# Five first pairs instead of six in a two-layer GELU block: the second and third range of the first weight prepared sooner, its factors on GpSimd

## The chip, the cores and the metric

The kernel runs on one core of one Trainium2 chip. The metric is device time in microseconds (us): the median over runs of the same kernel. Engines are named as in the profile: PE is TensorE's matmul, PEld its weight load, DVE is VectorE, ACT is ScalarE, POOL is GpSimd, SP is SyncE, which here only issues DMAs.

## The reference

`x` has 8 x 1024 rows of 1024, `w1` is 1024 x 4096, `w2` is 4096 x 1024, all float32.

```python
h = x @ w1
h = 0.5 * h * (1 + np.tanh(np.sqrt(2 / np.pi) * (h + 0.044715 * h ** 3)))
return (h @ w2).astype(np.float32)
```

## The kernel before

**Tiling.** The 8192 rows are 32 pairs of two blocks of 128 rows (`NP`). The 4096 columns of `w1` are two halves, and each half is cut into four ranges of 512 columns (`NR`). The unit of the first product is one pair and one range: two row blocks by two column halves, over two halves of the 1024 inner rows. That is a 2 x 2 by 2 x 2 block product. Done plainly (class `Plain`, L511) it takes 32 matmuls of 512 columns, in four quarters of eight. Done as `Quad1` (L540) it takes seven block products, m1 to m7, of four matmuls each, and needs sums of blocks on both sides: `sum_x` (L222) for x, and T1, T2, T3, T4 of the weight, made by `sum_w1` (L362).

**A range of w1** goes through these steps before it can be used: eight tiles of 512 KB are loaded by `load_w1` (L277; ranges 1 to 3 are issued by POOL, range 0 by SP), each tile is looked at for its largest value by `look_w1` (L291, on DVE or ACT), `widest_w1` (L306, DVE) takes the maximum per partition, `scale_w1` (L314) takes it over all partitions with one PE transposition into the tile `rows` (L158) followed by a DVE reduction, `factors` (L244) makes the scales for the GELU input and output, `cast_w1` (L348) makes float16 tiles, two tiles to each of the blocks B11, B21, B12 and B22, and `sum_w1` makes the T's. T4 takes the place of B12.

**A row block of x** is loaded (`load_x`, L181, SP), looked at (`look_x`, L185, ACT), scaled and cast (`cast_x`, L196), and turned, for the first pairs by eight PE transpositions and a copy out of PSUM (`turn_x_pe`, L206), later by a DMA.

**The order.** The first `FIRST` = 6 pairs are taken range by range: units 0 to 5 are range 0 done plainly, 6 to 11 are range 1, 12 to 17 range 2, 18 to 23 range 3, all as `Quad1`. Then come 22 middle pairs with all four ranges each, then the last four pairs range by range. Range 0 is cast with scales of its own halves for the plain units, and evened out in place (`even_w1`, L340, POOL) before the middle pairs use it. After 128 units the second product, with `w2`, follows.

**What sets the order on each engine.** Everything stands in the order in which it is written, and each engine runs its own queue strictly in that order. A plain quarter p is followed by GELUs of finished quarters and then by what was put at place p with `early`. In `unit` (L796) the steps of unit u stand between background slots 0 to 6; work is put there with `plan(u, slot, ...)`. The order inside one unit, which the prediction's steps use, is: m1 and its copy (ACT); slot 0; m7 of the unit before, its copy (ACT) and its addition (DVE); GELUs; slot 1; m3 of the unit two before and an addition (DVE); slot 2; m2 and an addition (DVE); slot 3; m6 (needs T2) and its copy (ACT); GELUs; slot 4; m5 (needs T1); slot 5; m4 of the unit before (needs T4); slot 6. The function `between(p)` (L915) puts the last x blocks and the second half of range 0 into the middle of the quarters 2 to 6. At p = 2 and p = 4, x blocks 5 and 7 are cast on POOL.

In the texts below T8, T9, T10 and T11 (with "x block") are the PE transpositions of x blocks 8 to 11, and q16 is the plain quarter 16; u7 is unit 7.

Of the kernel before, what the change touches and what calls it, by code (L numbers as in the profile page):

```python
# [31 lines left out]
B11, T4, B21, B22, T1, T2, T3 = range(7)  # L32
# [48 lines left out]
def kernel(  # L81
# [19 lines left out]
    NP = T // (2 * P)  # L101
    NR = I // 2 // N
    JR = N // P
    FIRST = 6
    LAST = 4
    OPEN = 4
    WARM = 52
# [3 lines left out]
    wpool = ctx.enter_context(tc.tile_pool(name="wpool", bufs=NR * 7))  # L111
    k4 = ctx.enter_context(tc.tile_pool(name="k4", bufs=15))
    k2 = ctx.enter_context(tc.tile_pool(name="k2", bufs=11))
    k1 = ctx.enter_context(tc.tile_pool(name="k1", bufs=8))
# [9 lines left out]
    xm = small.tile([P, T // P], F32, name="xm")  # L124
    xi = small.tile([P, T // P], F32, name="xi")
# [4 lines left out]
    w1m = small.tile([P, NR + 4], F32, name="w1m")  # L130
    w1i = small.tile([P, NR + 4], F32, name="w1i")
    w1j = small.tile([P, NR + 2], F32, name="w1j")
# [6 lines left out]
    us = small.tile([P, NP, 2, NR], F32, name="us")  # L139
    rs = small.tile([P, NP, 2, NR], F32, name="rs")  # L140
    rt = small.tile([P, T // P], F32, name="rt")
    up = small.tile([P, 3, 2 * FIRST], F32, name="up")
    ratio = small.tile([P, 4], F32, name="ratio")
# [4 lines left out]
    V, S, G = nc.vector, nc.scalar, nc.gpsimd  # L148
# [89 lines left out]
    def times(o, a, s, eng=V):  # L238
        if eng is G:
            G.tensor_scalar(out=o, in0=a, scalar1=s, scalar2=1.0, op0=ALU.mult, op1=ALU.mult)  # L240
        else:
            V.tensor_scalar(out=o, in0=a, scalar1=s, scalar2=None, op0=ALU.mult)

    def factors(k0, k1, r):  # L244

        c = slice(2 * k0, 2 * k1)
        view = lambda t: t[:, k0:k1].rearrange("p k h r -> p (k h) r")[:, :, r]
        times(view(us), xm[:, c], w1m[:, r:r + 1])
        times(view(rs), xi[:, c], w1j[:, r:r + 1])

    def ups_of_block(k, eng):
        c = slice(2 * k, 2 * k + 2)
# [206 lines left out]
    class Out1:  # L459


        def begin(self, k, r):
# [4 lines left out]
            if not r:  # L467
                self.v = [[self.v[h][0], rt[:, c(h)]] for h in range(2)]
            if not r and k < FIRST:
                self.u = [[(up[:, 0, c(h)], up[:, 1, c(h)]), up[:, 2, c(h)]] for h in range(2)]  # L470
# [206 lines left out]
    NQ = len(order)  # L677
    todo = {}

    def plan(u, slot, f, *args):  # L680
        assert 0 <= u, (f, args)
        todo.setdefault((u, slot), []).append((f, args))
# [6 lines left out]
    def early(p, f, *args):  # L689
        plan(p // 4, p % 4, f, *args)  # L690

    for k in range(OPEN, FIRST):
        for h in range(2):
            c = 2 * k + h
            p = (9, 12)[k - OPEN] + h
            early(p - 1, look_x, c)
            early(p, scale_x, c)
            early(p, cast_x, c, V)
            if h:
                early(p, factors_of_block, k, 0, G)  # L700
                early(p, factors_of_block, k, 1, G)
            early((2, 5)[k - OPEN], load_x, c, wpool, "w")
            early(4 * k - 2 + 2 * h - (k > 2), turn_x_pe, c, V if h else S)
    for k in first:
        for i in range(4):
            if k < 2:
                early((18, 21)[k] + i // 2, sum_x, k, (i,))
            else:
                plan(FIRST + k - 1, 2 + i, sum_x, k, (i,))

    for n in range(8):
        early((3, 4, 5, 6, 7, 8, 9, 10)[n], load_w1, 1, n)
        early((7, 8, 10, 12, 12, 13, 14, 15)[n], look_w1, 1, n, S if n in (3, 5, 7) else V)
    early(15, widest_w1, 1)
    early(17, scale_w1, 1)
    early(17, factors, 0, FIRST, 1)
    for i, n in enumerate((4, 5, 0, 1, 6, 7, 2, 3)):
        early((17, 17, 18, 18, 19, 19, 20, 21)[i], cast_w1, 1, n, S if i % 2 and n != 3 or n == 2 else V)
    early(20, sum_w1, 1, T1)
    early(22, sum_w1, 1, T2)  # L720
    plan(FIRST, 1, sum_w1, 1, T3)
    plan(FIRST, 5, sum_w1, 1, T4)
    for r in range(2, NR):
        u = (r - 1) * FIRST - 1
        for n in range(8):
            v = u - 1 + n // 2
            if r == 2:
                plan(*((4, 1), (4, 3), (5, 0), (5, 2))[n // 2], load_w1, r, n)
                look = ((5, 3), (6, 1), (6, 1), (6, 4), (6, 3), (7, 1), (7, 1), (7, 4))[n]
                plan(*look, look_w1, r, n, S if n % 2 else V)  # L730
            else:
                plan(v, 1, load_w1, r, n)
                look = (v + 2, 1) if n == 1 else (v + 1, 3 + n % 2)
                plan(*look, look_w1, r, n, S if n == 1 else V)
        plan(u + 3, 1 if r == 2 else 5, widest_w1, r)
        plan(*((u + 3, 6) if r == 2 else (u + 4, 2)), scale_w1, r)
        plan(u + 4, 2, factors, 0, FIRST, r)
        for n in range(8):
            v, slot = ((4, 3), (4, 4), (4, 5), (5, 1), (4, 3), (4, 5), (5, 3), (4, 6))[n]
            plan(u + v, slot, cast_w1, r, n, (G, S, G, S, G, V, S, V)[n])  # L740
        for i, t in enumerate((T1, T3, T2, T4)):
            plan(u + 5 + i // 2, (4, 6, 1, 3)[i], sum_w1, r, t)
    early(10, join_w1)
    for i, b in enumerate((B12, B11, B22, B21)):
        for half in range(2):
            plan(3 * FIRST - 1 + i, (2, 5)[half], even_w1, b, half)
    for i, t in enumerate((T1, T3, T2, T4)):
        plan(3 * FIRST + 1 + i, 5, sum_w1, 0, t)

    for k in list(middle) + list(last):  # L750
        a = at[k] if k in middle else at[last[0]]
        for h in range(2):
            c = 2 * k + h
# [10 lines left out]
    u = at[middle[0]] - 1  # L764
    for ic in range(2 * IK):
        t = 7 * u + ic * 35 // 8
# [6 lines left out]
    for c in range(8):  # L773
        v = u + 2 + c * 7
# [12 lines left out]
    for i, node in enumerate(FORMS):  # L787
        r, n = divmod(i, 7)
# [52 lines left out]
    with tc.manual_schedule(  # L841
# [18 lines left out]
        for n in range(4, 8):  # L860
# [5 lines left out]
        t = x16[0]  # L866
# [8 lines left out]
        warm_up(t, 8)  # L875
        cast_w1(0, 0, V)
        cast_w1(0, 1, V)
        plain = {k: Plain(k, 0) for k in range(FIRST)}
        pa, pc = bank("pa"), bank("pc")
        plain[0].eighth(0, 0, pa)  # L880
        look_w1(0, 2, S)
        scale_x(1)
        cast_x(1, V)
# [4 lines left out]
        warm_up(t, 3)  # L888
        turn_x_pe(1, V)
        scale_w1(NR + 3)  # L890
        plain[0].eighth(1, 0, pc)
        cast_w1(0, 2, V)
        cast_w1(0, 3, S)
        ups_of_block(0, G)
# [2 lines left out]
        look_x(3)  # L897
        join_halves()
        inverse_w1(slice(NR, NR + 1), G)
        plain[0].eighth(0, 1, pa)  # L900
        turn_x_pe(2, S)
        times(rs[:, 0, :, 0], xi[:, 0:2], w1j[:, NR:NR + 1], G)
        plain[0].eighth(1, 1, pc)
        scale_x(3)
        cast_x(3, V)
        look_x(4)
        look_x(5)
        quarters = [(k, 0, half, s) for s in range(2) for k in range(OPEN) for half in range(2)]
        quarters += [(k, 0, half, s) for k in range(OPEN, FIRST) for half in range(2) for s in range(2)]
        gelus = {  # L910
            0: lambda: plain[0].gelu(0, 0, plain[0].e(), pa),
            1: lambda: plain[0].gelu(1, 0, plain[0].e(), pc),
        }

        def between(p):  # L915
            if p == 2:
                scale_x(4)
                turn_x_pe(3, V)
                cast_x(4, V)
                scale_x(5)  # L920
                cast_x(5, G)
                gelus.pop(0)()
                factors_of_block(1, 0, G)
                look_x(6)
            elif p == 3:
                turn_x_pe(4, V)
                scale_x(6)
                look_w1(0, 4)
                gelus.pop(1)()
                factors_of_block(2, 0, G)  # L930
                look_x(7)
            elif p == 4:
                turn_x_pe(5, V)
                cast_x(6, V)
                scale_x(7)
                cast_x(7, G)
                look_w1(0, 5, S)
                gelus.pop(2)()
            elif p == 5:
                turn_x_pe(6, V)  # L940
                factors_of_block(3, 0, G)
                look_w1(0, 6)
                look_w1(0, 7, S)
                widest_w1(0, 1)
                gelus.pop(3)()
            elif p == 6:
                turn_x_pe(7, V)
                scale_w1(NR + 1)
                for n in range(4, 8):
                    cast_w1(0, n, S if n % 2 else V)  # L950
                inverse_w1(slice(NR + 1, NR + 2), G)
                for k in range(OPEN):
                    factors_of_block(k, 1, G)
                gelus.pop(4)()

        for p, (k, r, half, s) in enumerate(quarters):
            if p > 1:
                gelus[p] = plain[k].quarter(half, s, ("pa", "pc")[p % 2], lambda: between(p))
            if p > 6:
                for i in list(gelus)[:2]:  # L960
                    gelus.pop(i)()
            for j in (p % 4,) if p % 4 < 3 else (3, 4, 5, 6):
                background(p // 4, j)
            let_go(len(held) - 1 if len(held) > 1 and p % 2 else 0)
        now = {}
        for u in range(FIRST, NQ):
            unit(u, None)
        V.tensor_scalar(
            out=vo, in0=xm, scalar1=w2n, scalar2=SPAN, op0=ALU.mult, op1=ALU.mult
# [38 lines left out]
```

## Time and profile before

| what | number |
|---|---|
| median of 3 runs | 1530.53 us (1530.23 to 1531.13) |
| the profiled execution's own time | 1530.9 us |
| its span, first to last instruction | 1529.1 us |
| PE busy | 1521.4 us, 99% |
| DVE busy | 1176.3 us, 77% |
| ACT busy | 738.7 us, 48% |
| POOL busy | 478.1 us, 31% |
| granted TensorE clock | 1.00 |
| chain that ended last | PE 99%, DMA 1% |
| DMA, mean | 192 GB/s over the span, 330 GB/s from 20 to 50 us |

The span is the time between the first and the last instruction; the run's own time is 1.8 us longer, and the median of the runs lies 0.4 us under that run's time. A line of a timeline has the start in us, the time from start to end, the engine, the line of the kernel, the operation, what it writes and reads, and how many instructions were merged; a bracket at its end tells how long the engine was idle before and what ended that. "SPq" is the queue of SyncE. Two neighbouring instructions of one engine can overlap by some tens of ns, so in a full queue the distance from start to start is a little less than the duration.

### The profile page before, as it was taken

Reading aid. Unit: us, or ns where it says so; the run is one execution under the profiler, and the core shown is the slowest. Engines: PE = TensorE matmul, PEld = TensorE weight load, DVE = VectorE, ACT = ScalarE, POOL = GpSimd, SP = SyncE. Lnnn points to the kernel's source line nnn. Section 1 sums busy time; section 2 is a strip of 40 time slices with the busy share of each in tenths; the row PEclk is TensorE's granted clock in tenths of the full one; section 3 lists DMA queues with packets and bytes.
Section 4 is the critical chain, followed back from the end, with each engine's and each line's share of the span. In section 5 each row is a group of like instructions: output and inputs, shape, how many; then the busy total and the mean of one; then the engine's idle time right before and its main releaser. Section 6 shows DMA issues by size and latency. Waiting matters only on the chain.

```text
span 1529.1 us, 28771 instructions
## 1 busy us (share of the span) xinstructions
PE 1521.4 (99%) x10449; PEld 1018.4 (67%) x10449; DVE 1176.3 (77%) x2404; ACT 738.7 (48%) x1322; POOL 478.1 (31%) x604
## 2 busy tenths in 40 slices
PE   8999999999999999999999999999999999999999
PEld 5444444444444444444458888888888888888888
DVE  6886788777777777574348888888888888888886
ACT  7878778777777777787662111111111111111111
POOL 4789554555666666554440000000000000000000
PEclk9999999999999999999999999999999999999999
DMA  9764989888789788875995767767766866866873
GB/s 351 237 201 141 294 259 300 251 238 249 203 238 270 225 258 232 246 201 131 287 280 128 145 135 135 152 131 132 155 138 123 162 131 125 163 134 131 151 141 81
DMA packets 460991, 293.94 MB, mean 192 GB/s; under 512 B 334000, under 2 KB 429232, under 8 KB 460848
## 3 DMA queue, kind: packets, MB, share of 16 engines
q1 hardware_dynamic: 457392, 279.52, 72.5%
q0 software_dynamic: 3456, 12.58, 2.5%
q8 instruction: 81, 1.33, 0.4%
q14 instruction: 62, 0.51, 0.1%
HBM read 96.99 MB, written 114.29 MB: 138 GB/s over the span
## 4 chain that ended last, share of the span: by engine, by line
PE 99%; DMA 1%; ACT 0%; SPq 0%; issue 0%; DVE 0%; ACTq 0%
PE pa L438 53%; PE pc L438 31%; PE pb L438 14%; DMA xn<-in_x_dram 1%; PE turned L213 0%; SPq L286 0%; ACT junk L187 0%; ACT w L172 0%; ACT xT L218 0%; PE rows L158 0%; SPq L183 0%; DVE o L626 0%; ACT junk L302 0%; DVE w1a L312 0%; ACTq L483 0%
## 5 line engine op out<-in xcount | busy, mean ns | idle before, releaser
L438 PEld LDWEIGHTS <-gs 128*128 128x128 f16 x4608 | 450.8, 98 | 53.0 <-DVE gs L168 0.2
L174 POOL TENSOR_SCALAR g<-e,rs 128x512 f16<-128x512 f32 x446 | 364.2, 826 | 280.9 <-ACT e L483 247.7
L438 PEld LDWEIGHTS <-xs 128*128 128x128 f16 x1952 | 191.0, 98 | 229.7
L165 DVE TENSOR_TENSOR e<-pc,e 128x512 f32<-128x512 f32 x244 | 162.8, 686 | 204.0 <-ACT e L577 202.9
L438 PEld LDWEIGHTS <-xT 128*128 128x128 f16 x1672 | 162.8, 98 | 193.8 <-DVE xT L220 1.7
L438 PE MATMUL pa<-w,gs 128*128 128x256 f16 x2304 | 288.3, 273 | 0.0
L438 PE MATMUL pa<-w,xT 128*128 128x512 f16 (+1 forms) x1080 | 254.7, 377 | 0.5 <-ACT xT L218 0.2
L483 ACT ACTIVATE e<-e,us 128x512 f32<-128x512 f32 x366 | 251.2, 719 | 2.1 <-DVE e L165 2.0
L438 PE MATMUL pa<-w,xs 128*128 128x512 f16 x976 | 250.5, 379 | 0.0
L438 PE MATMUL pc<-w,xs 128*128 128x512 f16 x976 | 250.5, 379 | 0.0
L438 PEld LDWEIGHTS <-gT 128*128 128x128 f16 x2048 | 200.4, 98 | 23.2
L630 ACT ACTIVATE o<-pa,vo 128x256 f32<-128x256 f32 x96 | 45.2, 471 | 332.4 <-PE pa L438 332.4
L438 PE MATMUL pc<-w,gs 128*128 128x256 f16 x1536 | 193.8, 273 | 0.0
L438 PE MATMUL pa<-w,gT 128*128 128x256 f16 x1024 | 132.7, 273 | 0.0
L438 PE MATMUL pb<-w,xT 128*128 128x512 f16 x488 | 125.2, 379 | 0.0
L626 DVE SCALAR_TENSOR_TENSOR o<-pc,vo,o 128x256 f32<-128x256 f32 x160 | 77.1, 482 | 58.0 <-PE pc L438 58.0
L568 ACT COPY e<-pa 128x512 f32<-128x512 f32 x122 | 71.4, 585 | 91.1 <-PE pa L438 86.8
L168 DVE TENSOR_TENSOR gs<-gT,gs 128x1024 f16<-128x1024 f16 x160 | 109.8, 686 | 0.9 <-DMA gT<-gd 0.9
L626 DVE SCALAR_TENSOR_TENSOR o<-pa,vo,o 128x256 f32<-128x256 f32 x192 | 92.0, 480 | 19.3 <-PE pa L438 19.0
L438 PE MATMUL pc<-w,gT 128*128 128x256 f16 x768 | 99.5, 273 | 0.0
L438 PE MATMUL pb<-w,gs 128*128 128x256 f16 x768 | 99.5, 273 | 0.0
L558 ACT COPY e<-pa 128x512 f32<-128x512 f32 x122 | 70.5, 578 | 50.0 <-PE pa L438 49.0
(105 smaller groups left out, 1443.4 us busy)
## 6 DMA issues: line engine op xcount, KB each, us to landing
gd<-g SPq DMA_DIRECT2D x504, 128.0 KB, 3.3
wn<-in_w_dram SPq DMA_DIRECT2D x72, 512.0 KB, 5.1
xn<-in_x_dram SPq DMA_DIRECT2D x64, 512.0 KB, 5.8
out_dram<-o SPq DMA_DIRECT2D x62, 512.0 KB, 3.8
w<-wd SPq DMA_DIRECT2D x25, 512.0 KB, 5.9
wn<-in_w_dram POOLq DMA_DIRECT2D x24, 512.0 KB, 6.1
wd<-wt SPq DMA_DIRECT2D x24, 512.0 KB, 4.7
gT<-gd SPq DMA_TRANSPOSE x128, 6.3
```

Of the source, the lines that this page charges most:

```text
L165: V.tensor_tensor(out=o, in0=a, in1=b, op=ALU.add)
L168: V.tensor_tensor(out=o, in0=a, in1=b, op=ALU.subtract)
L174: G.tensor_scalar(out=o, in0=i, scalar1=s, scalar2=1.0, op0=ALU.mult, op1=ALU.mult)
L438: nc.tensor.matmul(bank, lhsT=left(i), rhs=right[i], start=start and i == 0, stop=i == n - 1, skip_group_check=True,)
L483: S.activation(out=e[:, c], in_=src[:, c], func=ACT.Gelu_apprx_tanh, scale=scale)
L558: S.copy(self.e11, self.pa)
L568: S.copy(self.e12, self.pa)
L626: V.scalar_tensor_tensor(out=o, in0=ps, scalar=v, in1=o, op0=ALU.mult, op1=ALU.add)
L630: S.activation(out=o, in_=ps, func=ACT.Copy, scale=v)
```

## The change

`FIRST` becomes 5. Only ten x blocks are then turned on PE. The quarters 0 to 19 are the five pairs on range 0; the quarters 20 to 23 are new and do pair 0 on range 1 plainly, so there are still six plain units. Unit 6 is now pair 1 on range 1, and there are 23 middle pairs. Range 1 is therefore needed from quarter 20, range 2 from unit 10 (before: 12), range 3 from unit 15 (before: 18), range 0 again from unit 20 (before: 24). The steps that prepare them are put sooner, and `factors` goes from DVE to POOL for ranges 1 to 3. One cast of range 3 stays on POOL where there were three.

```diff
-    FIRST = 6
+    FIRST = 5
...
-    def factors(k0, k1, r):
+    def factors(k0, k1, r, eng=V):
...
+        times(view(us), xm[:, c], w1m[:, r:r + 1], eng)
+        times(view(rs), xi[:, c], w1j[:, r:r + 1], eng)
...
-            if k < 2:
-                early((18, 21)[k] + i // 2, sum_x, k, (i,))
+            if k == 1:
+                early(22 + i // 2, sum_x, k, (i,))
             else:
-                plan(FIRST + k - 1, 2 + i, sum_x, k, (i,))
+                plan(FIRST - 1 + (k or FIRST), 2 + i, sum_x, k, (i,))
     for n in range(8):
-        early((3, 4, 5, 6, 7, 8, 9, 10)[n], load_w1, 1, n)
-        early((7, 8, 10, 12, 12, 13, 14, 15)[n], look_w1, 1, n, S if n in (3, 5, 7) else V)
+        early((3, 3, 3, 4, 4, 5, 5, 6)[n], load_w1, 1, n)
+        early((8, 9, 10, 11, 12, 13, 14, 14)[n], look_w1, 1, n, S if n % 2 else V)
     early(15, widest_w1, 1)
-    early(17, scale_w1, 1)
-    early(17, factors, 0, FIRST, 1)
-    for i, n in enumerate((4, 5, 0, 1, 6, 7, 2, 3)):
-        early((17, 17, 18, 18, 19, 19, 20, 21)[i], cast_w1, 1, n, S if i % 2 and n != 3 or n == 2 else V)
-    early(20, sum_w1, 1, T1)
-    early(22, sum_w1, 1, T2)
-    plan(FIRST, 1, sum_w1, 1, T3)
-    plan(FIRST, 5, sum_w1, 1, T4)
+    early(15, scale_w1, 1)
+    early(15, factors, 0, FIRST, 1, G)
+    for n in range(8):
+        early(16 + n // 2, cast_w1, 1, n, S if n % 2 else V)
+    for i, t in enumerate((T1, T2, T3, T4)):
+        plan(*((4, 3), (5, 0), (5, 1), (6, 1))[i], sum_w1, 1, t)
     for r in range(2, NR):
         u = (r - 1) * FIRST - 1
...
             if r == 2:
-                plan(*((4, 1), (4, 3), (5, 0), (5, 2))[n // 2], load_w1, r, n)
-                look = ((5, 3), (6, 1), (6, 1), (6, 4), (6, 3), (7, 1), (7, 1), (7, 4))[n]
+                early((10, 11, 12, 13, 14, 15, 16, 17)[n], load_w1, r, n)
+                look = ((5, 0), (5, 0), (5, 1), (5, 1), (5, 3), (5, 3), (6, 1), (6, 1))[n]
...
-        plan(u + 3, 1 if r == 2 else 5, widest_w1, r)
+        u -= r == 2
+        plan(*((u + 3, 3) if r == 2 else (u + 3, 5)), widest_w1, r)
         plan(*((u + 3, 6) if r == 2 else (u + 4, 2)), scale_w1, r)
-        plan(u + 4, 2, factors, 0, FIRST, r)
+        plan(u + 4, 2, factors, 0, FIRST, r, G)
...
-            plan(u + v, slot, cast_w1, r, n, (G, S, G, S, G, V, S, V)[n])
+            plan(u + v, slot, cast_w1, r, n, ((G, S, G, S, G, V, S, V), (V, S, G, S, V, V, S, V))[r - 2][n])
         for i, t in enumerate((T1, T3, T2, T4)):
             plan(u + 5 + i // 2, (4, 6, 1, 3)[i], sum_w1, r, t)
...
-            plan(3 * FIRST - 1 + i, (2, 5)[half], even_w1, b, half)
+            plan(3 * FIRST + i, (2, 5)[half], even_w1, b, half)
     for i, t in enumerate((T1, T3, T2, T4)):
-        plan(3 * FIRST + 1 + i, 5, sum_w1, 0, t)
+        plan(3 * FIRST + (2, 3, 4, 4)[i], (1, 1, 0, 4)[i], sum_w1, 0, t)
...
+        plain[0, 1] = Plain(0, 1)
...
+        quarters += [(0, 1, half, s) for half in range(2) for s in range(2)]
...
-        for u in range(FIRST, NQ):
+        for u in range(FIRST + 1, NQ):
```

More of the change, by code (lines that the diff above doesn't have):

```diff
@@ L242, in times @@
             V.tensor_scalar(out=o, in0=a, scalar1=s, scalar2=None, op0=ALU.mult)
-    def factors(k0, k1, r):
+    def factors(k0, k1, r, eng=V):
         c = slice(2 * k0, 2 * k1)
         view = lambda t: t[:, k0:k1].rearrange("p k h r -> p (k h) r")[:, :, r]
-        times(view(us), xm[:, c], w1m[:, r:r + 1])
-        times(view(rs), xi[:, c], w1j[:, r:r + 1])
+        times(view(us), xm[:, c], w1m[:, r:r + 1], eng)
+        times(view(rs), xi[:, c], w1j[:, r:r + 1], eng)
     def ups_of_block(k, eng):
@@ L694 @@
             c = 2 * k + h
-            p = (9, 12)[k - OPEN] + h
+            p = 9 + h
             early(p - 1, look_x, c)
@@ L701 @@
                 early(p, factors_of_block, k, 1, G)
-            early((2, 5)[k - OPEN], load_x, c, wpool, "w")
+            early(2, load_x, c, wpool, "w")
             early(4 * k - 2 + 2 * h - (k > 2), turn_x_pe, c, V if h else S)
@@ L877 @@
         cast_w1(0, 1, V)
-        plain = {k: Plain(k, 0) for k in range(FIRST)}
+        plain = {(k, 0): Plain(k, 0) for k in range(FIRST)}
+        plain[0, 1] = Plain(0, 1)
         pa, pc = bank("pa"), bank("pc")
-        plain[0].eighth(0, 0, pa)
+        plain[0, 0].eighth(0, 0, pa)
         look_w1(0, 2, S)
@@ L890 @@
         scale_w1(NR + 3)
-        plain[0].eighth(1, 0, pc)
+        plain[0, 0].eighth(1, 0, pc)
         cast_w1(0, 2, V)
@@ L899 @@
         inverse_w1(slice(NR, NR + 1), G)
-        plain[0].eighth(0, 1, pa)
+        plain[0, 0].eighth(0, 1, pa)
         turn_x_pe(2, S)
         times(rs[:, 0, :, 0], xi[:, 0:2], w1j[:, NR:NR + 1], G)
-        plain[0].eighth(1, 1, pc)
+        plain[0, 0].eighth(1, 1, pc)
         scale_x(3)
@@ L909 @@
         quarters += [(k, 0, half, s) for k in range(OPEN, FIRST) for half in range(2) for s in range(2)]
+        quarters += [(0, 1, half, s) for half in range(2) for s in range(2)]
         gelus = {
-            0: lambda: plain[0].gelu(0, 0, plain[0].e(), pa),
-            1: lambda: plain[0].gelu(1, 0, plain[0].e(), pc),
+            0: lambda: plain[0, 0].gelu(0, 0, plain[0, 0].e(), pa),
+            1: lambda: plain[0, 0].gelu(1, 0, plain[0, 0].e(), pc),
         }
@@ L957 @@
             if p > 1:
-                gelus[p] = plain[k].quarter(half, s, ("pa", "pc")[p % 2], lambda: between(p))
+                gelus[p] = plain[k, r].quarter(half, s, ("pa", "pc")[p % 2], lambda: between(p))
             if p > 6:
```

## The prediction

> **What bounds the kernel now.** I read first the page's chain that ended last (PE 99%), then the windows of 10 us, then PE's waits, then the timelines of PE, POOL, DVE and ACT from 24 to 96 us. PE is busy without a gap from about 17 us to the last products. It works at a fixed beat: a plain quarter starts every 1.73 us, a full Quad1 unit every 6.04 us, so four matmuls take 0.86 us of its queue. All that PE ever waits for by name is this:
>
> ```profile
> engine line waited for: us in total, times, longest us
> PE pb L451 <- DVE identity L857: 1.6, 1, 1.6
> PE rows L158 <- DVE w1a L312: 1.6, 3, 0.9
> ```
>
> So whatever the change takes off DVE, ACT, POOL or the DMA queues is worth nothing by itself. Only PE's own queue and new waits of PE count. Here is the stretch around range 1's transposition, PE alone:
>
> ```profile
> 45.58 0.61 PE L213 MATMUL turned<-identity,x 128*128 128x128 f16 x8
> 46.02 1.89 PE L438 MATMUL pa<-w,xT 128*128 128x512 f16 x8
> ...
> 49.48 0.61 PE L213 MATMUL turned<-identity,x 128*128 128x128 f16 x8
> 50.47 0.29 PE L158 MATMUL rows<-identity,w1a 128*128 128x128 f32 x1 [0.39 <-DVE w1a L312]
> 50.60 1.89 PE L438 MATMUL pa<-w,xT 128*128 128x512 f16 x8
> ...
> 54.06 0.61 PE L213 MATMUL turned<-identity,x 128*128 128x128 f16 x8
> 54.51 1.89 PE L438 MATMUL pa<-w,xT 128*128 128x512 f16 x8
> ```
>
> These are T9 and q16, T10, rows of range 1, q18, T11 and q20. Turning an x block costs PE 0.44 (45.58 to 46.02). Rows costs 0.13, and it waited 0.56 in all: 49.48 + 0.43 = 49.91 to 50.47.
>
> **The change, part by part.** Products on PE: none added or removed (six plain units both times). The beat stays.
>
> *1. Two turned blocks fewer.* T10 and T11 go: 0.43 + 0.45 = **-0.88**.
>
> *2. Three range-1 loads ahead of x block 7's cast on POOL.* Before, one load stands there:
>
> ```profile
> 24.90 0.70 POOL L240 TENSOR_SCALAR rs<-xi,w1j 128x2 f32<-128x2 f32 x1
> 25.54 0.89 POOL L286 DMA_DIRECT2D wn<-in_w_dram  x1
> 26.49 1.11 POOL L174 TENSOR_SCALAR x<-xn,xi 128x1024 f16<-128x1024 f32 x1
> 27.59 0.68 POOL L174 TENSOR_SCALAR g<-e,rs 128x512 f16<-128x512 f32 x1
> 28.22 0.75 POOL L286 DMA_DIRECT2D wn<-in_w_dram  x1
> ```
>
> Each issue holds POOL 0.72 to 0.89 (24 of them, median 0.75). Two more move the cast's end from 27.60 to 29.10. T7, the next thing in PE's queue, stood at 27.99 and now starts at 29.10. After it, rows of range 0 waited for DVE until 28.60 and no longer has to, so the quarter behind starts 28.73 -> 29.66: **+0.93**. POOL is then some 3 us late, with four more issues. Behind it stand GELU multiplications and the scales of block 1. The GELU of q8 needs those at about 35.8 and has them at 34.8, and PE's banks reach back six quarters, so this costs nothing; without that cover it would be 1 us.
>
> *3. Rows of range 1 directly behind T9.* The loads are no longer late. But in DVE's queue the copy of T9 out of PSUM now stands ahead of `widest_w1`, and PE's next instruction is rows. From T9's start: 0.65 until the copy starts (54.06 to 54.71), 0.60 to DVE's next start (54.71 to 55.31), 0.31 from w1a to rows (50.16 to 50.47) = 1.56, where PE is ready at 0.44. Wait 1.12 instead of 0.56: **+0.56**. T9 moves to 45.58 + 0.93 = 46.51, rows to 48.07, q16 to 48.20, q20 to 55.11, u6 to 62.01 (before 61.41).
>
> *4. Rows of range 2 at the end of u6, behind a full DVE queue.* Before, it stood at the end of u8 (76.09) and waited for nothing. The DVE and ACT rows that carry this step:
>
> ```profile
> 57.09 1.21 DVE L168 TENSOR_TENSOR w<-w 128x2048 f16<-128x2048 f16 x1
> ...
> 61.08 1.71 DVE L168 TENSOR_TENSOR w<-w 128x2048 f16<-128x2048 f16 x1
> 62.71 1.21 DVE L151 TENSOR_REDUCE w1c<-wn 128x1 f32<-128x1024 f32 x1
> 63.84 1.21 DVE L168 TENSOR_TENSOR w<-w 128x2048 f16<-128x2048 f16 x1
> 64.97 1.21 DVE L151 TENSOR_REDUCE w1c<-wn 128x1 f32<-128x1024 f32 x1
> 66.10 0.68 DVE L165 TENSOR_TENSOR e<-pb,e 128x512 f32<-128x512 f32 x1
> ```
> ```profile
> 55.01 0.71 ACT L483 ACTIVATE e<-pc,up 128x512 f32<-128x512 f32 x1
> 55.58 1.18 ACT L172 ACTIVATE w<-wn,w1i 128x1024 f16<-128x1024 f32 x1
> 56.62 0.87 ACT L483 ACTIVATE e<-pa,up 128x256 f32<-128x256 f32 x2
> ```
>
> A T and a look each take 1.13 start to start. The addition at 66.10 is of a product whose last matmul ended at 63.30: DVE is already 2.8 us behind here, with nobody waiting. After the change PE waits. The last cast of range 1 on ACT stands behind the GELU of q19: q19 starts at 53.38 and its results are there 1.89 later (55.27), GELU 0.57 start to start, cast 1.18: 57.05. T2 needs it. Then DVE has in its order T2, look, T3, look, four sums of x, look, T4, look, sum, addition, sum, widest: 7 x 1.13 = 7.9, six sums 2.1 (0.33 to 0.45 each), addition 0.60, and 0.31 to rows: 10.9. Rows at 57.05 + 10.9 = 68.0. PE reaches it after four quarters and u6, which has no older unit's products in it (16 matmuls): 62.01 + 3.45 = 65.46. **+2.5**. Nothing hides it. It is nought if DVE is 2.5 us quicker, and more if POOL hinders DVE.
>
> A sub beside POOL's multiplications took 1.71 here and 1.21 elsewhere (mean of 11: 1.32). The Trainium skill, "SBUF — State Buffer", section "Who interferes with whom", says that a DVE instruction with two SBUF inputs contends with a GpSimd instruction that reads SBUF, and that one fully blocks the other. The trace agrees in part: some are longer by 0.5, most by nothing. What this would make is a rival below, worked out from the rows.
>
> *5. The sums of range 3 with one unit less in hand.* They stand at units 14 and 15 and are needed in 15; before at 16 and 17 for 18. T2 (slot 1 of u15) stands behind the addition of m7's product, and this behind m7's copy on ACT. In the ordinary case the copy starts 1.98 after the unit's start (88.29 -> 90.27), ends at 2.56, addition 0.60, T2 1.21: 4.4, and m6 needs it at 16 matmuls = 3.45: 1.0. But ACT has two casts of range 3 in u14, as in u10 before, and now also a look at x (`look_x`, slot 5), since the first middle pair's preparation falls there:
>
> ```profile
> 85.90 2.19 ACT L172 ACTIVATE w<-wn,w1i 128x1024 f16<-128x1024 f32 x2
> 87.98 0.58 ACT L568 COPY e<-pa 128x512 f32<-128x512 f32 x1
> 88.44 1.35 ACT L483 ACTIVATE e<-e,us 128x512 f32<-128x512 f32 x2
> 89.68 0.58 ACT L558 COPY e<-pa 128x512 f32<-128x512 f32 x1
> 90.27 0.58 ACT L577 COPY e<-pa 128x512 f32<-128x512 f32 x1
> ```
>
> Here ACT was just in time with no look. A look adds 1.04, so m7's copy starts at about 2.9 instead of 1.98, and T2 ends at 5.35: **+1.9**, with 1.0 as the lower bound by these rows (nought if DVE and ACT come early), and 2.4 if T3 also runs long.
>
> *6. The rest.* `factors` on POOL: 0.34 + 0.25 off DVE per range, POOL 0.3 to 0.7 more, needed a unit later: 0. Casts of range 3 from POOL (1.33 each) to DVE: covered, DVE has some 2 us free in unit 13. Evening range 0: 1.11 per half on POOL beside four multiplications of 0.7 to 0.9, ready half a unit ahead: 0; uncovered, up to 1. Range 2's loads sooner: the two looks that waited for them (0.33 and 1.21) no longer wait, off PE's path.
>
> *Sum.* -0.88 + 0.93 + 0.56 + 2.5 + 1.9 = **+5.0**. On the profiled run's 1530.9 (span 1529.1 and 1.8 around it) this is 1535.9; the median is 0.4 lower, so **1535.5 us** on its scale.
>
> **The rivals.**
>
> *A. The queues are not late (not slower).* If DVE starts widest of range 2 before 65.15, PE waits for nothing at rows; and if m7's copy is early, u15 costs at most 1.0. Both gone: -0.88 + 0.93 + 0.56 = +0.6, 1531.1; without step 2's and 3's waits too, and with the 0.56 at rows saved, -1.4, 1529.1. For it: all steps come sooner, and POOL takes two operations per range from DVE. Against: ten microseconds of DVE work have 8.4 us of room. Chance 0.12.
>
> *B. Only one large wait comes.* Without step 4: 1533.0; without step 5: 1533.6. Chance 0.10 each.
>
> *C. Range 1's loads land late.* Eight are issued in 12 us instead of 18. The median from issue to landing is 6.4, the longest 12.1. The last one, issued at about 37.2, is due for its look at 45.9; at 12.1 it comes 3.4 late, and rows, which have 0.7 to spare behind that look, 2.7 later: 1538.2. Against: two x loads (1 MB) go away just before, and the mean from 20 to 50 us was 330 GB/s while the early peak is 400. Chance 0.12.
>
> *D. POOL blocks DVE in step 4.* Three T's 0.5 longer each: 1537.0. Chance 0.11.
>
> **How the numbers follow.** Forecast 0.45, A 0.12, B 0.20, C 0.12, D 0.11. 0.2% of the median is 3.1 us, about what a measurement of this kernel can tell from no change, so "slower" begins at 1533.6. Faster needs less than 1527.5, which no case gives: 0.01. Same: A 0.11, the first of B 0.10, half of the second 0.05 = 0.26. Slower 0.73. The range 1531.5 to 1538.5 leaves out most of A and the worst of C, under 0.2.
>
> **What would show it.** In the changed profile: T7 waiting for POOL's cast, about 1.1 us; rows waiting for w1a about 1.1 behind T9 and 2.5 at about 65 us; m6 of u15 waiting for DVE's w (PE pa <- DVE w, L168) about 1.9 near 120 us; nothing later. If PE's waits total as before, I am wrong in steps 2 to 5. If rows waits for ACT or a DMA instead, C holds.

## The result, and the profile after

The changed kernel takes **1538.65 us** (median of 6 runs, 1537.74 to 1540.0) against 1530.62 us (6 runs, 1530.23 to 1531.26): ratio **1.0053**, interval 1.0042 to 1.0064. That is slower, as forecast, but 0.15 us above the upper end of the range. Its profiled execution is the fastest of the six: 1537.74 us, span 1535.9.

The first and the last microseconds differ from run to run, so I compare the *middle*: from the first plain products of 512 columns (17.99 before, 17.62 after) to the start of the last products (1524.90, 1531.33). It grew from 1506.91 to 1513.71, by 6.80 us, and it is given below for most experiments.

What PE waits for, by name, in the changed kernel (total, times, longest; the five largest rows):

```profile
PE rows L158 <- DVE w1a L312: 4.3, 4, 2.5
PE pa L438 <- DVE w L168: 1.8, 1, 1.8
PE pb L451 <- DVE identity L856: 1.6, 1, 1.6
PE pa L438 <- ACT e L558: 1.2, 1, 1.2
PE turned L213 <- POOL x L174: 1.1, 1, 1.1
```

The third is the start. The others are where the forecast put them, except the fourth. Their places on PE's timeline:

```profile
28.84 0.62 PE L213 MATMUL turned<-identity,x 128*128 128x128 f16 x8 [1.10 <-POOL x L174]
...
46.26 0.61 PE L213 MATMUL turned<-identity,x 128*128 128x128 f16 x8
47.73 0.32 PE L158 MATMUL rows<-identity,w1a 128*128 128x128 f32 x1 [0.86 <-DVE w1a L312]
47.89 1.89 PE L438 MATMUL pa<-w,xT 128*128 128x512 f16 x8
...
61.70 1.03 PE L438 MATMUL pa<-w,xT 128*128 128x512 f16 x4
62.56 1.03 PE L438 MATMUL pb<-w,xT 128*128 128x512 f16 x4
64.78 1.02 PE L438 MATMUL pa<-w,xs 128*128 128x512 f16 x4 [1.19 <-ACT e L558]
65.64 1.03 PE L438 MATMUL pc<-w,xs 128*128 128x512 f16 x4
69.17 0.32 PE L158 MATMUL rows<-identity,w1a 128*128 128x128 f32 x1 [2.50 <-DVE w1a L312]
69.33 1.03 PE L438 MATMUL pa<-w,xT 128*128 128x512 f16 x4
...
122.44 1.04 PE L438 MATMUL pa<-w,xs 128*128 128x512 f16 x4 [1.79 <-DVE w L168]
```

These are, in order: T7; T9, rows of range 1 and q16; u6 with m1, m2, m6, m5; rows of range 2 and u7; m6 of u15. After that PE never waits again. u6 has 16 matmuls, 3.45 us, and rows 0.13: from 61.70 u7 could start at 65.28. It starts at 69.33. Step 4 cost **4.05 us where 2.5 was forecast**. Two things were not in the forecast. First DVE's queue on the way to rows, and POOL's beside it:

```profile
55.24 3.21 DVE L168 TENSOR_TENSOR w<-w 128x2048 f16<-128x2048 f16 x2 [2.80 <-ACT w L172]
58.38 1.21 DVE L151 TENSOR_REDUCE w1c<-wn 128x1 f32<-128x1024 f32 x1
59.51 1.91 DVE L168 TENSOR_TENSOR w<-w 128x2048 f16<-128x2048 f16 x1
...
62.91 0.80 DVE L168 TENSOR_TENSOR xs<-xs,xT 128x512 f16<-128x512 f16 x1
...
68.96 0.15 DVE L312 TENSOR_REDUCE w1a<-w1c 128x1 f32<-128x12 f32 x1
```
```profile
56.48 0.89 POOL L174 TENSOR_SCALAR g<-e,rs 128x512 f16<-128x512 f32 x1
57.37 1.64 POOL L174 TENSOR_SCALAR g<-e,rt 128x512 f16<-128x512 f32 x1
58.99 1.35 POOL L174 TENSOR_SCALAR g<-e,rs 128x512 f16<-128x512 f32 x2
```

T1 takes 1.58, T2 (from 56.91) 1.54, T3 1.91, a sum 0.80, where the forecast had 1.21 and, for a sum, 0.41 (0.33 to 0.45 from start to start). From T2 on that is 1.42 more. The look between them, which has one input, keeps its 1.21. T2 starts while the first of POOL's multiplications shown runs and ends 1.08 after it (57.37 to 58.45); T3 starts while the last two run and also ends 1.08 after them (60.34 to 61.42). The multiplication from 57.37 in turn runs beside T2 and takes 1.64, where an undisturbed one takes 0.69. Second, ACT is late with m1's copy, for which m6 waits:

```profile
61.96 0.69 ACT L483 ACTIVATE e<-pc,us 128x512 f32<-128x512 f32 x1 [1.04 <-PE pc L438]
63.10 1.06 ACT L302 ACTIVATE junk<-wn 128x1024 bf16<-128x1024 f32 x1 [0.46 <-DMA gd<-g]
64.07 0.19 ACT L302 ACTIVATION_READ_ACCUMULATOR junk<-wn 128x1 f32 x1
64.16 0.57 ACT L558 COPY e<-pa 128x512 f32<-128x512 f32 x1
```

The copy stands behind a look, and the look behind a store: its output buffer is one that a GELU result still holds.

### The profile page after: what moved, and what is told of

Its sections match the earlier page's. It is cut to its first block, busy times and chain, and to the rows that moved or that the text cites. A ratio compares the mean times of both kernels' runs of the same rounds, so it can differ in the third digit from the quotient of the medians.

```text
span 1535.9 us, 28743 instructions
## 1 busy us (share of the span) xinstructions
PE 1520.6 (99%) x10433; PEld 1016.3 (66%) x10433; DVE 1179.6 (77%) x2403; ACT 738.7 (48%) x1321; POOL 474.9 (31%) x603
## 4 chain that ended last, share of the span: by engine, by line
PE 95%; ACT 2%; DVE 1%; DMA 1%; issue 0%; POOL 0%; SPq 0%; ACTq 0%; DVEq 0%
PE pa L438 51%; PE pc L438 30%; PE pb L438 14%; ACT e L483 1%; DMA xn<-in_x_dram 1%; DVE w L168 0%; ACT w L172 0%; DVE w1c L151 0%; ACT junk L187 0%; ACT junk L302 0%; ACT xT L218 0%; PE turned L213 0%; SPq L286 0%; POOL wn L286 0%; DVE xs L168 0%
## 5 line engine op out<-in xcount | busy, mean ns | idle before, releaser
L174 POOL TENSOR_SCALAR g<-e,rs 128x512 f16<-128x512 f32 x446 | 360.3, 817 | 290.0 <-ACT e L483 273.3
```

What stands on the lines that cost most here:

```text
L174: G.tensor_scalar(out=o, in0=i, scalar1=s, scalar2=1.0, op0=ALU.mult, op1=ALU.mult)
```

## Experiments

Each ratio is against the kernel before on the same chip, so it stands by itself. Edits are against the changed kernel. *Step 4's cost* is, in every run, from where u7 could start (3.58 after u6's start) to where it starts; in the changed kernel it is 4.05.

### Step 4: the wait at rows of range 2

**Widest of range 2 right behind its looks, T4 of range 1 behind it.**

```diff
-        plan(*((u + 3, 3) if r == 2 else (u + 3, 5)), widest_w1, r)
+        plan(*((u + 3, 1) if r == 2 else (u + 3, 5)), widest_w1, r)
-        plan(*((4, 3), (5, 0), (5, 1), (6, 1))[i], sum_w1, 1, t)
+        plan(*((4, 3), (5, 0), (5, 1), (6, 4))[i], sum_w1, 1, t)
```

> The changed kernel with two places moved: the widest of range 2 stands directly behind its looks (slot 1 of unit 6), and T4 of range 1 behind it (slot 4). If the length of DVE's queue ahead of the widest sets the long wait of PE before rows of range 2 (the changed kernel's 69.17 us, wait 2.50), rows comes 1.13 (T4) + 0.33 + 0.60 + 0.35 (sum, addition, sum) sooner, about 66.9, and the time falls by 2.2 to 2.4 us. If the looks on ACT or their loads set it, rows stays near 69 and the time falls by less than 0.5 us.

Measured 1535.33 us, ratio 1.003 (1.0019 to 1.0042); middle 1511.39, 2.32 less. Rows waited 0.82 and m6 0.68; step 4 cost 1.86. T1 to T3 were as long as before (3.23 for the first two, then 1.91) and nothing was taken off any engine: what stands ahead of widest in DVE's queue sets when rows can start.

**POOL's multiplications replaced by writes.** This kernel leaves out a part of the output, where it writes zeros.

```diff
-            cast(G, g[:, s], e, self.v[half][s])
+            G.memset(g[:, s], 0.0) if self.k in (0, OPEN) else cast(G, g[:, s], e, self.v[half][s])
```

> The changed kernel with GpSimd's GELU multiplications of pairs 0 and 4 (on range 1 and 0 in the quarters 16 to 23, and in later units of pairs 0 and 4 nothing else) replaced by writing zeros, so that part of the output is left out: GpSimd still writes there but reads nothing. If GpSimd's reads hinder DVE's instructions with two inputs, the T's and sums between 55 and 64 us shrink from 1.6, 1.9 and 0.8 to 1.2, 1.2 and 0.4, rows of range 2 comes 1.2 to 1.5 sooner, and the time falls by as much. If they were long for another reason, they stay and the time changes by less than 0.3.

Measured 1536.23, ratio 1.0035 (1.0023 to 1.0048); middle 1512.13. POOL's writes and DVE's T2 beside them in that trace:

```profile
55.61 2.87 POOL L491 MEMSET g<- 128x512 f16 x6
```
```profile
56.52 1.23 DVE L168 TENSOR_TENSOR w<-w 128x2048 f16<-128x2048 f16 x1 [0.39 <-ACT w L172]
```

T2 takes 1.23 although POOL writes all the while. T3 (58.80, 1.22) and the sum (0.42) are short as well, but POOL does nothing beside them, since the writes are over at 58.48. Step 4 cost 2.59. So it was POOL's multiplications that made them long, and T2 shows that POOL's writing alone does not; what is left is its reading. The Trainium skill, "SBUF — State Buffer", section "Who interferes with whom", says that this pair shares one read interface and that the order of issue decides which of the two is held up. The traces agree: in the changed kernel T2 and T3 end 1.08 after the multiplications that they found running; in the next run T2 starts first and keeps 1.24, and it is POOL's multiplication that takes 1.64 instead of 0.69.

**Factors back on DVE**, one part of the change undone.

```diff
-    early(15, factors, 0, FIRST, 1, G)
+    early(15, factors, 0, FIRST, 1)
-        plan(u + 4, 2, factors, 0, FIRST, r, G)
+        plan(u + 4, 2, factors, 0, FIRST, r)
```

> The changed kernel with the factors of ranges 1 to 3 back on DVE, one part of the change undone. Theory (step 6: 0.34 and 0.25 us per range beside PE's path are worth nothing): as the changed kernel, 1537.7 to 1538.7. Rival (POOL was the better place, since DVE's chain to rows of range 2 has no slack): range 1's factors put DVE's casts, and with them T1 to T4 and rows of range 2, up to 0.6 later, and the time rises by as much.

Measured 1536.35, ratio 1.0037 (1.0025 to 1.005); middle 1512.41, 1.30 less; step 4 cost 2.86. Neither theory had that. POOL and DVE in that trace:

```profile
57.74 1.64 POOL L174 TENSOR_SCALAR g<-e,rt 128x512 f16<-128x512 f32 x1
```
```profile
57.58 1.24 DVE L168 TENSOR_TENSOR w<-w 128x2048 f16<-128x2048 f16 x1 [0.39 <-ACT w L172]
...
59.88 1.25 DVE L168 TENSOR_TENSOR w<-w 128x2048 f16<-128x2048 f16 x1
```

T2 starts first, so the multiplication waits and T2 does not. In the changed kernel the factors of range 1 hold POOL for 0.93 us (51.87 to 52.80); here they hold DVE for 0.27 (49.41 to 49.68). Counted from the first plain products (17.62 and 18.35) the multiplications beside T1 and T2 start 0.4 to 0.6 sooner here, and T1 starts when it did before (37.62 in both), T2 0.06 sooner. So T1 no longer finds a multiplication running. That the shift turns the order round is read from this one trace.

**Loads of range 2 issued by SyncE instead of POOL.**

```diff
-        (G if r else nc.sync).dma_start(
+        (G if r in (1, 3) else nc.sync).dma_start(
```

> The changed kernel with the eight loads of range 2 issued by SyncE instead of POOL; each issue holds POOL for 0.75 us, so POOL is freed of 6 us between 44 and 57 us. Theory (POOL's queue, with sixteen load issues and the factors in it, is behind both parts of step 4 that were not in the forecast: its GELU multiplications come late enough to lie beside T2 and T3 on DVE, and the stores that follow them hold back the buffer that m1's copy on ACT needs): T1, T2, T3 take 1.2 each instead of 1.6, 1.6 and 1.9, m6 of unit 6 waits 0 to 0.6 instead of 1.19, rows of range 2 waits about 2 with DVE's chain alone; 1535.8 to 1536.6 and no clock below 1. Rival (POOL's load issues have nothing to do with it, or SyncE's queue holds the stores back instead): m6's wait stays at 1.2 or grows, the time stays at 1537.7 to 1538.7 or more.

Measured 1536.3, ratio 1.0039 (1.0026 to 1.0052); middle 1512.42. PE and DVE:

```profile
64.09 1.02 PE L438 MATMUL pa<-w,xs 128*128 128x512 f16 x4 [0.62 <-ACT e L558]
...
67.86 0.32 PE L158 MATMUL rows<-identity,w1a 128*128 128x128 f32 x1 [1.88 <-DVE w1a L312]
```
```profile
56.70 1.23 DVE L168 TENSOR_TENSOR w<-w 128x2048 f16<-128x2048 f16 x1 [0.40 <-ACT w L172]
...
58.98 1.21 DVE L168 TENSOR_TENSOR w<-w 128x2048 f16<-128x2048 f16 x1
```

With POOL's six microseconds of issues (POOL was busy 29.5 of the 30 us from 30 to 60, and is now 23.7) the T's are short again, and m6's wait is 0.62 instead of 1.19. The two waits sum to 0.62 + 1.88 = 2.50 against 3.69 in the changed kernel. Counted as the forecast counts it, step 4 cost 2.86, as with the factors on DVE; one sum is still long in both (0.70 here, 0.60 there, for 0.41). So POOL's queue is the common cause of both extras. One run of the five had a mean clock of 0.999.

**One look of range 2 on ACT a slot sooner.**

```diff
-                look = ((5, 0), (5, 0), (5, 1), (5, 1), (5, 3), (5, 3), (6, 1), (6, 1))[n]
+                look = ((5, 0), (5, 0), (5, 1), (5, 1), (5, 3), (5, 2), (6, 1), (6, 1))[n]
```

> The look at tile 5 of range 2 goes on ACT from slot 3 of unit 5 to slot 2. In the changed kernel's profile it stood there, held back by the store of another tile, ahead of m1's copy of unit 6, for which m6 waited 1.19 us. Theory (rows of range 2 is set by DVE's chain from T2 on, and m6's wait lies inside the same time): m6's wait may go or shrink, rows then waits as much longer, 2.50 to about 3.7, time 0 +- 0.3. Rival (the wait for ACT adds to the one for DVE): the two together fall from 3.7 to 2.5 and the time by 1.2.

Measured 1537.82 (1536.94 to 1539.63), ratio 1.005 (1.0037 to 1.0062). m6 still waited 1.12: now a GELU ahead of m1's copy waited 1.54 for a store. The theory holds in that the time stayed; what it said of the look did not matter, since the buffer is held whoever asks for it.

### The other steps

**Range 1's loads behind x block 7's cast** (step 2).

```diff
-        early((3, 3, 3, 4, 4, 5, 5, 6)[n], load_w1, 1, n)
+        early((4, 4, 4, 4, 4, 5, 5, 6)[n], load_w1, 1, n)
```

> The changed kernel with the first three loads of range 1 put one quarter later, so that on POOL the cast of x block 7 stands ahead of all loads. If the loads ahead of this cast make T7 wait, its 1.10 us wait goes, and the time falls by 0.9 (rows of range 0 then waits for DVE again for some 0.2). If the early issue of these loads is needed, a look of range 1 becomes late and rows of range 1 takes the gain back: no change or slower.

Measured 1536.39, ratio 1.0036 (1.0022 to 1.005); middle 1512.16. T7's wait is gone, and the quarter behind it starts 10.69 after the first plain products (before 10.74, changed kernel 11.79). T2 and T3 took 1.2 here as well, as POOL's order had shifted against DVE's, but two sums took 1.11 and 0.83, so step 4 still cost 3.72.

**The copy of x block 9 on ACT** (step 3).

```diff
-            early(4 * k - 2 + 2 * h - (k > 2), turn_x_pe, c, V if h else S)
+            early(4 * k - 2 + 2 * h - (k > 2), turn_x_pe, c, S)
```

> The copy of x block 9 out of PSUM goes from DVE to ACT, so that it no longer stands ahead of widest of range 1 in DVE's queue. Theory (step 3: the copy is what rows of range 1 waits for): T9 to q16, 1.63 us in the changed kernel's profile, falls by about one copy, 0.5 to 0.6, to 1.1; the wait in the row "rows <- DVE w1a" near 47.7 falls from 0.86 to 0.3. But the gain then meets rows of range 2, which is bound by DVE's own chain: if that chain does not start sooner, PE waits there the 0.5 longer and the time stays (0 to -0.2); if the chain does start sooner with the casts of range 1, -0.5. Rival (rows of range 1 is bound by the looks, not by the copy): the wait stays at 0.86 and the time as well.

Measured 1536.19, ratio 1.0036 (1.0023 to 1.0049); middle 1512.09.

```profile
46.62 0.61 PE L213 MATMUL turned<-identity,x 128*128 128x128 f16 x8
47.51 0.32 PE L158 MATMUL rows<-identity,w1a 128*128 128x128 f32 x1 [0.28 <-DVE w1a L312]
```

The wait fell from 0.86 to 0.28, as step 3 wants it. Most of the rest of the 1.62 us comes from step 4, which cost 3.13 with a T2 and T3 of 1.25.

**T2 of range 3 ahead of T3** (step 5).

```diff
-        for i, t in enumerate((T1, T3, T2, T4)):
+        for i, t in enumerate((T1, T3, T2, T4) if r == 2 else (T1, T2, T3, T4)):
```

> The changed kernel with T2 and T3 of range 3 exchanged in order (T2 in slot 6 of unit 14, T3 in slot 1 of unit 15). If T2 is late because it stands in DVE's queue behind the addition of m7 in unit 15, PE's wait for DVE's w near 122 us (1.79) goes, and nothing else becomes late: the time falls by 1.9. If a cast on ACT or POOL were what T2 waits for, the wait stays and the time is the same.

Measured 1539.04 (1536.91 to 1540.76), ratio 1.0051 (1.0039 to 1.0064): inconclusive as a time, since four of its five runs, the profiled one among them, had a mean clock of 0.998 or 0.999. The time did not fall by the expected 1.9. In the trace the wait in u15 is gone (m2 at 123.20, m6 at 124.07). But PE waits 1.27 in u20, at 155.72, for m1's copy on ACT, where the changed kernel did not: of the 1.96 won, 0.69 stays.

**One look at x a unit sooner** (step 5).

```diff
-            plan(a - 6 + late + h, 5, look_x, c)
+            plan(a - 6 + late + h - (c == 2 * FIRST), 5, look_x, c)
```

> One look at x (the first of the first middle pair) goes from unit 14 to unit 13, so that ACT has two casts and no look there; the order of the T's stays. Theory (step 5: ACT is late by that look, 1.04 us, and with it m7's copy, the addition and T2): m7's copy starts 1.9 to 2.0 after the start of unit 15 instead of 2.90, the gap from m2 to m6 of unit 15 falls from 1.96 to about 1.0, time -0.9 (some 1536.8 against a profile of 1537.7). Rival (T2 is late because of DVE's own queue): the gap stays at 1.9 to 2.0 and the time too.

Measured 1537.92, ratio 1.0051 (1.0038 to 1.0063). Expected 0.9, got a gap of 1.47 instead of 1.96 (121.45 to 123.78, less the 0.86 of four matmuls). ACT has no free moment from 113.8 to 122: the look went to another place in the same full queue. So step 5's size is right, but it is ACT's whole load from u13 on that makes it, not that look alone.

**Products of the identity in the place of the wait.**

```diff
+            if r == 2: plan(u + 3, 6, warm_up, identity16, 40)
```

> The changed kernel with 40 products of the identity (128 columns each, about 2.2 us, result not used) on PE ahead of rows of range 2, so that PE waits at most 0.4 us there instead of 2.5. Nothing that is computed changes, and rows is where DVE's chain puts it. Theory (PE's long wait lets its granted clock fall to 0.50 for some 3.3 us in about half of the executions, which costs 1.6 us): no run with a mean clock of 0.998 or 0.999, all of them 1537.0 to 1538.3, median 0.5 to 0.9 under the changed kernel's 1538.65. Rival (the slower runs have another cause, such as the start): about half of the runs stay at 1539 and more with a clock below 1.

Measured 1537.98 (1537.61 to 1539.75), ratio 1.0051 (1.0037 to 1.0064). Rows still starts where DVE lets it (69.09). One run of five had a clock of 0.999, against three of six. The theory had expected none, and so few runs can't decide it.

### All orders together

**Four orders** (widest sooner, loads behind the cast, T2 ahead of T3, copy on ACT; the four edits above).

> All four orders together: widest of range 2 right behind its looks with T4 of range 1 behind it, the first three loads of range 1 behind x block 7's cast, T2 of range 3 ahead of T3, the copy of x block 9 on ACT. Theory (the waits of PE are the whole loss): of the changed kernel's profiled 1537.7, T7's wait 0.9, rows of range 1 0.5, rows of range 2 2.3 to 4.0 and m6 of unit 15 2.0 go: 1530.3 to 1532.0, within 0.1% of the kernel before (five pairs first are then worth no more than the two turned blocks, 0.88). Rival (something else than these waits costs time, such as the DMA traffic or more instructions): it stays over 1533 with PE's waits gone.

Measured 1534.48, ratio 1.0026 (1.0016 to 1.0036); middle 1510.56. It missed the 1530.3 to 1532.0: the old waits are gone or small, and these came in their place:

```profile
63.85 1.02 PE L438 MATMUL pa<-w,xs 128*128 128x512 f16 x4 [2.06 <-ACT e L558]
...
87.44 1.04 PE L438 MATMUL pa<-w,xs 128*128 128x512 f16 x4 [0.88 <-DVE xs L168]
...
149.43 1.02 PE L438 MATMUL pa<-w,xs 128*128 128x512 f16 x4 [1.27 <-ACT e L558]
```

A wait of PE gives all other engines time. Once it is gone, the next one is late.

**The same with three repairs.**

```diff
-  look = ((5, 0), (5, 0), (5, 1), (5, 1), (5, 3), (5, 3), (6, 1), (6, 1))[n]
+  look = ((5, 0), (5, 0), (5, 1), (5, 1), (5, 3), (6, 1), (6, 1), (6, 1))[n]
-                plan(FIRST - 1 + (k or FIRST), 2 + i, sum_x, k, (i,))
+                plan(FIRST - 1 + (k or FIRST), 2 + i - 2 * (k == 4), sum_x, k, (i,))
-    u = at[middle[0]] - 1
+    u = at[middle[0]]
...
-    u += 20
+    u += 19
```

> The four orders of the run before and four more, for the waits that were new there: the look at tile 5 of range 2 goes on ACT behind m1's copy of unit 6 (m6 there waited 2.06 us for that copy); the sums of x of pair 4 go two slots sooner (m6 of unit 9 waited 0.88 for one); the looks at w2 start one unit later (m6 of unit 20 waited 1.27 for ACT, which waited for DVE). Theory (each wait is a matter of order in one queue): all three go, 4.2 us, and the time is 1530.0 to 1531.0, level with the kernel before or up to 0.5 below it. Rival (DVE is full from 55 to 90 us, 36 of 40 us busy and without a break from 70 on; the order only decides which of PE's instructions waits): what is taken from m6 of unit 6 comes back as a wait for DVE in units 7 to 10, and the time stays over 1532.

Measured 1531.76 (11 runs, 1531.41 to 1533.23), ratio 1.0009 (1.0000 to 1.0018); middle 1509.23 in its profiled execution, the longest of the eleven. This is above the expected 1530.0 to 1531.0 and under the rival's 1532. The waits in u9 and u20 are gone (0.18 left), so they were no sign of a DVE that is simply full; m6 of u6 still waits 1.53 for ACT, and ACT for a store.

**The same with the factors on DVE and range 2's loads on SyncE.**

> The eight orders of the run with all repairs, the factors back on DVE, and the loads of range 2 on SyncE. Theory (with POOL relieved, m6 of unit 6 no longer waits 1.5 us for ACT, and rows of range 2 no longer 0.4): of 1531.76 some 1.2 to 1.9 go: 1529.9 to 1530.6, level with the kernel before (1530.7) or up to 0.8 below it, which is all that two turned blocks fewer can give. Rival (DVE is full, the waits come back): 1531.5 to 1532.5.

Measured **1531.02** (11 runs, 1530.81 to 1531.47), ratio **1.0003** (0.9994 to 1.0012): level with the kernel before, 0.4 above what was expected. The middle is 1506.98 against 1506.91. PE's waits by name:

```profile
PE rows L158 <- DVE w1a L312: 2.1, 4, 1.1
PE pb L451 <- DVE identity L856: 1.6, 1, 1.6
PE turned L213 <- ACT x L172: 0.8, 1, 0.8
PE pb L451 <- DVE w1m L162: 0.4, 1, 0.4
PE pa L438 <- ACT e L558: 0.3, 1, 0.3
```

Most of that is the start. From start to start PE loses 0.43 at rows of range 1 (45.57 + 0.44 = 46.01 to 46.44), 0.62 at rows of range 2 (63.00 + 0.86 to 64.48) and 0.44 in u20 (145.04 + 0.86 to 146.34): 1.49. The kernel before lost 0.56, and two turned blocks save 0.88: 1.49 - 0.56 - 0.88 = 0.05, and the middle differs by 0.07. No version was faster than the kernel before.

## Why the prediction was right, and where it failed

The forecast was 1535.5, and 3.15 us too low. Of that 1.8 lie in the middle (6.80 instead of 5.0), 1.55 of it in step 4; 1.3 lie in the median, which the forecast put 0.4 below the profiled execution and which is 0.9 above it. Either one alone would have left the time inside the range.

| step | forecast | measured, from PE's timeline |
|---|---|---|
| 2: T7 behind the loads | +0.93 | +1.05 (11.79 - 10.74) |
| 3: rows of range 1 behind T9 | +0.56 | +0.50 (30.27 - 28.03 = 2.24 to q16, less 1.05, less the 0.69 that rows cost before) |
| 4: rows of range 2 behind DVE's queue | +2.5 | **+4.05** (69.33 - 65.28; its two brackets sum to 3.69, and each wait costs some 0.2 more than its bracket) |
| 5: m6 of u15 behind T2 | +1.9 | +1.96 (122.44 - 120.48) |

With the -0.88 of step 1 this is 6.68; the middle grew by 6.80.

**Right:** the place and the releaser of every wait but m6's in u6, and four of five sizes (step 1's is taken as forecast). Step 5's count for m7's copy, "about 2.9" after the unit's start, was 2.90 (117.03 to 119.93):

```profile
118.43 1.05 ACT L187 ACTIVATE junk<-xn 128x1024 bf16<-128x1024 f32 x1
...
119.93 0.60 ACT L577 COPY e<-pa 128x512 f32<-128x512 f32 x1
```
```profile
120.56 0.69 DVE L165 TENSOR_TENSOR e<-pc,e 128x512 f32<-128x512 f32 x1 [2.48 <-ACT e L577]
121.17 1.22 DVE L168 TENSOR_TENSOR w<-w 128x2048 f16<-128x2048 f16 x1
```

**Failed: step 4's term "2.5", and step 6's "factors on POOL: 0" with it.** The sum took 1.13 for a T and 0.33 to 0.45 for a sum. In the changed kernel POOL's multiplications run when T2, T3 and a sum of x start, and these three take 1.42 more than in the forecast, of the 1.55 by which the term was too small. In the run in which POOL only writes they keep the forecast's durations, and step 4 costs 2.59. What put the multiplications there is POOL's queue, with sixteen load issues of 0.75 and the factors: with the factors back on DVE, or with range 2's loads on SyncE, step 4 costs 2.86 and the middle is 1.3 less (1512.41 and 1512.42). By these figures it is one effect, not two: either edit takes most of it away. It was rival D, with too small a chance. That D's price (1.5) came out is in part luck, since it was made up of three T's 0.5 longer each and not of two T's 0.33 and 0.70 longer and a sum 0.39 longer. Step 6 had charged POOL's extra work at nothing because its result is needed only a unit later. The wait for ACT (1.19) is not an extra cost beside it: PE would have waited for DVE in that time anyway; it becomes the bound only when DVE's chain is shortened (2.06 with the four orders).

**Not in the forecast at all: the median lies 0.9 above the profiled execution.** Three of the six runs had a mean clock of 0.999, and they took 1539.51 on average; the others, with 1.000, took 1537.96. A trace shows what that can be. In the run with one look of range 2 sooner, PE's clock (the column behind POOL's) after the wait at rows:

```profile
68.00:70.00 2.00, 0.65 (x4) 0.40 (x5) 2.00 (x7) 0.00 (x0) 0.00 (x0) 1.00 0.00 0
70.00:72.00 2.00, 2.00 (x7) 0.78 (x6) 0.48 (x3) 0.59 (x1) 0.00 (x0) 0.54 0.00 0
72.00:74.00 2.00, 2.00 (x7) 0.67 (x6) 0.80 (x2) 1.21 (x2) 0.12 (x1) 0.61 0.00 0
74.00:76.00 2.00, 2.00 (x11) 0.93 (x10) 2.00 (x6) 1.09 (x2) 2.00 (x4) 1.00 0.17 57
```

Over two windows the clock averages 0.54 and 0.61, which is 0.50 for some 3.4 us. Meanwhile four matmuls take up to 1.91 instead of 1.03, and 1.7 us are lost: the twelve from 69.51 to 73.79 take 4.28 instead of 2.59. The run with T2 first and the one with the look at x sooner show the same at the same place; the changed kernel's own trace does not, though its pause is no shorter. So a wait of PE of this length can cost more than its length. The three slower runs of the changed kernel, 1.55 longer than the others, fit this loss, but none of them was traced.

**Open:** in how many executions this happens. Of the 21 runs of these four kernels 12 had a mean clock under 1, but a mean of 0.999 does not prove a pause. The traced execution with the four orders has 0.999, yet its clock is full up to the last products, whose last start is at 1528.08, and falls only behind them, where it costs no product any time:

```profile
1520.00:1529.00 9.00, 9.00 (x84) 1.00 0.20 67
1531.00:1532.70 1.70, 0.00 (x0) 0.54 0.00 0
```

The run with T2 first had 0.83 from 10 to 20 us too, after a wait of 1.89 for the first weights. It is also open whether DVE or POOL is held up in each execution of one kernel; only one execution of each was traced.

## What to carry to other kernels

An engine that nobody waits for still has a price: work given to it shifts its other instructions, and where these hold up a full engine, as POOL's multiplications held up DVE here, that engine pays. When a preparation is put sooner, sum the queue of each engine up to the instruction that PE waits for, and then ask what is late next; here three waits had successors of 0.9 to 2.1 us. A stall of PE can be worth removing beyond its length: in three traces here its clock fell after it.

## What the runs showed of the hardware that was not expected

- **The granted clock can fall to half at a short pause.** In the three traces that show it, the products stood still for 2.4 to 3.3 us (the shortest from 66.99, where m5's four matmuls are through, to 69.35), with another wait of 0.6 to 1.1 just before. The Trainium skill, "TensorE: Matmul & The Clock Gate", section "Why this matters for your kernels", advises against idle gaps over some 3 us. The traces differ in the size: 2.4 was enough, with the other wait before it; and in the changed kernel's trace 2.7 at the same place did nothing. Runs with a mean clock under 1 were 12 of 21 for the four kernels with such a pause, two of nine with one of 2.2 (the four orders), and one of 53 for the eight kernels whose traces have none over 2.05 once the start is over.
- **Which of DVE and POOL is held up depends on who starts first.** In the changed kernel's trace T2 and T3, started beside a running multiplication, took 1.54 and 1.91; with the factors on DVE T2 started first and took 1.24, and the multiplication behind it 1.64 instead of 0.69.
- **A load issue holds the queue that issues it.** Each held POOL's for 0.72 to 0.89, 0.75 in the middle; when SyncE issued the eight of range 2 between its stores instead, no new wait of PE came of it.
